# Twelve merged tiles turned by VectorE blocks and a DRAM round trip, and SyncE's queue written out by the planner

## The chip, the cores and the metric

The kernel runs on one core of a Trainium2 chip, in one launch. The metric is the device time of that core in microseconds (us). It was 1301.48 us before, the median of 3 runs from 1300.34 to 1301.94 us.

## The reference

One layer of a hybrid encoder on `x` of 512 tokens by 2048 features, in float32:

```python
hn = rmsnorm(x, norm_g)
proj = hn @ w_in                      # 12 q,k,v,gate groups of 4x128 columns, 4 forget logits, 3x2048 gate logits
gates = sigmoid(proj[gate columns] + b_gate)          # 3 branches x 2048
ya = forgetting_attention(...)        # 4 heads of 128: causal softmax with cumulative log forget bias
yb = chunked_relpos_attention(...)    # 4 heads: band of chunks with a learned relative bias
yc = stick_breaking_attention(...)    # 4 heads: causal, in log space
ys = stack(ya, yb, yc) * silu(gate)
up = einsum('bsnw,nwd->bsnd', ys, w_up)               # each branch 512 -> 2048
merged = sum(gates * up, over the 3 branches)
return x + merged @ w_out
```

`merged` is made with tokens on the partitions and columns on the free axis. The output projection contracts over the columns, so it needs them on the partitions: `merged` has to be turned.

## The kernel before

**Tiles and stages.** Every float32 product on PE is made of three products of split operands: a high part times the whole (high and low) of the other, and a low part times the high one. A weight block `raw` (128 partitions x 1024) is loaded by SyncE, its high part `wh` is made by ACT (L376), its low part `wl` by DVE (L386), and PE multiplies (L266). One such block is a *unit*: 12 matmuls of 512 columns in the Strassen-like projections, 24 in the others. `prep` readies units two ahead (`LA = 2`). There are 405 units in a row: the first head's group and gate group, then 11 heads of 28 units (attention of one head runs beside the projection of the next), then the up projections of 24 units, then the output projection of 2 x 28 units.

**The up stage.** `merged` has 4 column groups `g` of 512 columns and 4 token blocks `tb` of 128. The groups run in the order 0, 2, 1, 3. For each, three branches of two units are multiplied; `gates_of` loads the spilled gate logits (`sg<-gl`) and applies a sigmoid, `taken` multiplies and adds on DVE (L1323, L1330), and after the third branch `merged[g, tb]` is complete. `turned_m(g, i)` then makes the four tiles `m` of the group, each with 128 columns on the partitions and 512 tokens free: four PE transposes into one PSUM bank (L1357) and one copy on ACT (L1364). `merged_a` and `merged_b` make the operands of the output projection out of `m`: groups 0 and 1 give the `m1` operands, which the first units of the output projection read (group 0 first, group 1 from the fifth unit on); groups 2 and 3 are combined with them into `m2`, `m23` and `m4`.

**The heads' gate path.** `Head.gate` turns the gate columns of all heads but the last without PE: DVE transposes 32x32 blocks (L920), SyncE stores the tile to a DRAM scratch `gd` (L923), and ACT's queue issues four reads that put the blocks in place (L930). `silu` uses the result about ten units later.

**What sets the order.** A planner (`Flow`) simulates the work as generators: each yields an engine with a cost, an event to wait for, or slots of a buffer pool (`t2s`: 20 SBUF tiles, `raws`: 8 weight blocks, `atts` and `accs`: 4 PSUM banks each). The task that can start first, then the one due first, is taken and its instructions are emitted; that order is final on PE, ACT and DVE (`manual_schedule`). DMAs cost the planner nothing on an engine: `fetch` issues on SyncE and estimates the landing, `stored` estimates when a stored tile is free again. The order on SyncE's queue is not the planner's: the framework sets it. A queue issues in order, and an instruction that waits holds up what is behind it.

Of the kernel before, what the change touches and what calls it, by code (L numbers as in the profile page):

```python
# [15 lines left out]
P = 128  # L16
# [20 lines left out]
Q, K, V, G = 0, 1, 2, 3  # L37
PE, ACT, DVE = 0, 1, 2

# [25 lines left out]
class Flow:  # L65
# [4 lines left out]

    LATE = (0.3, 0.12, 0.12)

    def __init__(self):
        self.clock = [0.0] * 3
        self.idle = [0.0] * 3
        self.now = self.fin = 0.0
        self.tasks = []
# [86 lines left out]
def hybrid_kernel(  # L164
# [103 lines left out]

    line = [0.0, 0.0]

    def landing(ready, kb):

        line[0] = max(line[0], ready) + 0.5
        line[1] = max(line[1], line[0] + 1.0) + kb / 370.0
        return line[1] + 1.5

    def fetch(to, src, ready, kb):
        nc.sync.dma_start(to, src)
        return Event(landing(ready, kb))

    def add_up(to, src, ready, kb):
        nc.gpsimd.dma_start(to, src, accum_op=ALU.add)  # L282
        line[1] += kb / 250.0
        return Event(max(line[1], ready) + 6.5)

# [42 lines left out]
    for c in (0, 2):  # L328
# [18 lines left out]
    class Unit:  # L347
# [7 lines left out]
        def load(self):  # L355
            for s in self.srcs:
                yield raws, 1
                self.raw = raw_tile(self.shape)
                self.there.t = fetch(self.raw, s, flow.ready, 256 * self.shape[0]).t

# [192 lines left out]
    class Product(Unit):  # L553
# [6 lines left out]
        def load(self):  # L560
            task, p, c = self.task, self.p, self.c
            if p in (3, 6):
                return
            yield raws, 1
            self.raw = raw_tile()
            first, more = {1: ((0, 0), None), 2: ((0, 1), None), 4: ((1, 1), None),
                           5: ((1, 1), (1, 0)), 7: ((0, 0), (1, 0))}[p]
            ev = fetch(self.raw, task.src(*first, c), flow.ready, 512)
# [25 lines left out]
    class Strassen:  # L594
# [36 lines left out]
        def left(self, name, tb, op):  # L631

            if self.rest is None:
                set_(self.event(name, tb))
                return
            yield t2s, 1
            r = t2("xr")
            yield fetch(r, self.rest(name, tb), flow.now, 256)
# [76 lines left out]
    def forget_weights():  # L715

        yield t2s, 1
        t = t2("fw")
        yield fetch(t[:NH * KT, :2 * P], wfg, flow.now, 64)
        yield DVE, 0.25  # L720
        nc.vector.tensor_mul(t[:NH * KT, :P], t[:NH * KT, :P], t[:NH * KT, P:2 * P])
        nc.sync.dma_start(fwd.rearrange("h (k p) -> (h k) p", p=P), t[:NH * KT, :P])
        stored(t2s, 1, 32)
        fw_ev.t = flow.fin + 4.0

    def forget_sums(c, pair):

        yield f_sums[2 * c + pair - 1] if c + pair else fw_ev
        yield t2s, 2
        hs = range(2 * pair, 2 * pair + 2)  # L730
        ws = [t2("fb") for _ in hs]
        ev = [fetch(w, fwd[h:h + 1, c * S:(c + 1) * S].to_broadcast([P, S]), flow.now, 256) for w, h in zip(ws, hs)]
        yield t2s, 2
        xs_ = []

        def ahead(tb):
            x = t2("xf")
            t = fetch(x, xn[tb, c], flow.now, 256).t
            xs_.append((x, Event(max(ev[1].t, t) + FLATE)))

        ahead(0)
        ahead(1)
        for tb in range(QB):
            x, there = xs_[tb]
            yield there
            yield atts, 1
            for w, h, to in zip(ws, hs, (att(), x)):
                yield DVE, dve_us(S) + 0.12
                nc.vector.tensor_tensor_reduce(out=to, in0=x, in1=w, scale=1.0, scalar=0.0, op0=ALU.mult, op1=ALU.add,
                                               accum_out=fl[:, tb, h, c:c + 1])  # L750
                if to is not x:
                    give(atts)
            if tb + 2 < QB:
                ahead(tb + 2)
            else:
                give(t2s)
        give(t2s, 2)
        set_(f_sums[2 * c + pair])

    def forget_bias():  # L760
# [19 lines left out]
        give(atts)  # L780
        nc.sync.dma_start(fd.rearrange("b h p -> (b h) p"), t[:T, :P])
        stored(t2s, 1, 16)
        for h in range(NH):
            nc.sync.dma_start(v[32 * h:32 * (h + 1), :], fd[:, h, :].rearrange("b (c t) -> b c t", t=T))
        yield Event(flow.fin + 8.0)
        q = 0.15
# [19 lines left out]
        nc.vector.tensor_add(v, v, p)  # L806
        nc.sync.dma_start(fd2.rearrange("h (c t) -> (h c) t", t=T), v)
        f2_ev.t = flow.fin + 3.0

# [7 lines left out]
    class Head:  # L817
# [95 lines left out]
        def gate(self):  # L913
            yield from self.all_there()
            yield t2s, 1
            if not self.last:
                t = t2("gt")
                for tb in range(QB):
                    yield DVE, 0.3
                    nc.vector.transpose(t[:, blk(tb)], self.c[tb][:, blk(G)])  # L920
                self.taken()
                gd = dp.tile([4 * QB, 32, P], F32, name=nm("gd"))
                nc.sync.dma_start(gd.rearrange("(t a) r c -> (a r) t c", a=4), t.rearrange("p (t c) -> p t c", t=QB))  # L923
                stored(t2s, 1, 256)
                yield Event(flow.fin + 12.0)
                yield t2s, 1
                yield ACT, 0.2
                t = self.t[G] = t2("g")
                for b in range(4):
                    nc.scalar.dma_start(t[32 * b:32 * (b + 1), :].rearrange("p (n c) -> p n c", c=32),  # L930
                                        gd.rearrange("n r (b c) -> b r n c", c=32)[b])
                self.event(G).t = flow.fin + 14.0
                return
# [20 lines left out]
        def soft_start(self):  # L954
# [3 lines left out]
            if n == A:  # L958
                yield f2_ev
                b = self.bias = t2("cr")  # L960
                ev = fetch(b, fd2[self.h:self.h + 1, :].to_broadcast([P, S]), flow.now, 256)
                yield ev
# [3 lines left out]
            else:  # L966
                self.bias = t2("tb")
                ev = fetch(self.bias, rel[self.h], flow.now, 256)
                yield ev
# [125 lines left out]
        def av(self, j):  # L1095
# [23 lines left out]
            if not self.last:  # L1119
                yd[self.n, self.h] = dp.tile([P, S], F32, name=nm("yd"))  # L1120
                nc.sync.dma_start(yd[self.n, self.h], self.y)
                stored(t2s, 1, 256)

# [25 lines left out]
    def brow(i):  # L1149
        yield t2s, 1  # L1150
        b = brows[i] = t2("bg")
        brow_ev[i].t = fetch(b, b_gate[i:i + 1, :].to_broadcast([P, S]), flow.now, 256).t

    brows, brow_ev, brow_used = {}, {i: Event() for i in range(NB * NQ)}, {}

    def spill(i, tb, c, src):
# [9 lines left out]
        gl[key] = dp.tile([P, S], F32, name=nm("gl"))  # L1166
        nc.sync.dma_start(gl[key], c)
        stored(t2s, 1, 256)

# [107 lines left out]
    def split_y(i):  # L1277
        def go():
# [6 lines left out]
            else:  # L1285
                yield heads[i].event("y")
                yield t2s, 1
                t = t2("yr")
                yield fetch(t, yd[n, h], flow.now, 256)
            yield from split(ys[i].hi, ys[i].lo, two(t), S, y_ev[i])  # L1290
# [9 lines left out]
    def gates_of(n, g, tb):  # L1300
        yield last_head.event("hl", 2)
        yield t2s, 1
        t = sig[n, g, tb] = t2("sg")
        yield fetch(t, gl[n, g, tb], flow.now, 256)
        yield last_head.event("g")
# [42 lines left out]
    kept_m, m1_ev, mus = {}, [Event() for _ in range(UK)], {}  # L1348

    def turned_m(g, i):  # L1350
        for tb in range(QB):
            yield merged_ev[NB - 1, g, tb]
# [12 lines left out]
        give(atts)  # L1365
        k = 4 * g + i
        if k < UK:
            kept_m[k] = m
            spawn(merged_a(k, m), 4.0, flow.fin)
        else:  # L1370
            spawn(merged_b(k - UK, m), 3.0, flow.fin)

# [47 lines left out]
    for g in (0, 2, 1, 3):  # L1420
# [40 lines left out]
    def loads():  # L1461
        def x(kt):
# [4 lines left out]
            xraw[kt] = t2("x")  # L1467
            x_in[kt].t = fetch(xraw[kt], xT[kt], 0.0, 256).t

        def n(i):  # L1470
            n_in[i].t = fetch(xnat[i // 2][:, i % 2, :], xn[i // NQ, i % NQ], 0.0, 256).t

# [6 lines left out]
        for kind, i in order:  # L1479
            if kind == "x":  # L1480
                yield from x(i)
            elif kind == "n":
                n(i)
            else:
                yield from units[i].load()
# [18 lines left out]

    line[0] = 0.8
    flow.fin = 4.0
# [14 lines left out]
NR = 8  # L1521

OFF = dict(cs=4, ct=12, co=14, s=8, t=14, o=16, s1=3, t1=4, o1=5)
FAT, FGAP, FLATE = 44, 15, 3.5
# [49 lines left out]
```

## Time and profile before

| What | us |
|---|---|
| median of 3 runs | 1301.48 |
| the runs | 1301.48, 1300.34, 1301.94 |
| span of the profiled execution | 1300.1 |
| PE busy in it | 1294.1 |
| DVE busy | 1069.5 |
| ACT busy | 748.2 |
| POOL busy | 92.0 |

The page gives the profiled execution's time as its span, from first to last instruction; what lies around it is not listed, and the runs lie 0.2 to 1.8 us above it. Matmuls are pipelined and overlap, so a row's mean duration (about 390 ns for one of 512 columns) is longer than the distance from one to the next. "PEld" is PE's weight load, "SPq" SyncE's queue, "ACTq" the queue of ACT. In a row of waits stand the waiter, the releaser, then us in total, times and the longest. In a row of DMA issues stand the transfer, its queue, the count, the KB of each and the median us from issue to landing. The granted clock was 1.000 throughout.

### The profile page before, as it was taken

To read this page: it belongs to the slowest core of one execution; us is meant where nothing else is said; L and a number is where in the kernel's file an instruction comes from. 1 tells how busy PE (TensorE), PEld (TensorE's weight loads), DVE (VectorE), ACT (ScalarE), POOL (GpSimd) and SP (SyncE) were. 2 spreads that over 40 slices of the span, in tenths; PEclk is the share of its full clock that TensorE was granted. 3 is DMA by queue.
4 is the path that set the end of the run, shared out by engine and by line. 5 is a ranking of instruction groups with operands and counts; after the bars stand their busy time and mean duration, and the time that the engine had idled before them with its cause. 6 is when DMAs were issued, how large, how long until landed. Compare 5 with 4: busy or idle time off the path is not lost.

```text
span 1300.1 us, 17368 instructions
## 1 busy us (share of the span) xinstructions
PE 1294.1 (100%) x5941; PEld 1075.1 (83%) x5941; DVE 1069.5 (82%) x1607; ACT 748.2 (58%) x1259; POOL 92.0 (7%) x116
## 2 busy tenths in 40 slices
PE   9999999999999999999999999999999999999998
PEld 8888888888888888888888888888888888888887
DVE  7966797898989888898886886978879668698767
ACT  7745465565557646576466664666658546463442
POOL 0001000110011001110011000110000000000110
PEclk9999999999999999999999999999999999999999
DMA  9855687896788989888787777877796756738983
GB/s 358 256 147 145 185 230 194 230 239 215 218 238 237 250 236 272 236 240 240 205 249 175 222 213 191 252 162 208 224 282 194 264 194 196 177 93 258 250 245 126
DMA packets 124072, 284.39 MB, mean 219 GB/s; under 512 B 34368, under 2 KB 40144, under 8 KB 123984
## 3 DMA queue, kind: packets, MB, share of 16 engines
q1 hardware_dynamic: 83328, 221.42, 50.7%
q0 software_dynamic: 14976, 54.53, 23.1%
q10 hardware_dynamic: 25680, 7.34, 2.3%
q8 instruction: 46, 0.75, 0.2%
q14 instruction: 42, 0.34, 0.1%
HBM read 260.66 MB, written 22.59 MB: 218 GB/s over the span
## 4 chain that ended last, share of the span: by engine, by line
PE 99%; DMA 1%; DVE 0%; issue 0%; ACT 0%; ACTq 0%
PE acc L266 93%; PE att L1019 1%; PE att L873 1%; DMA gl<-u 1%; PE att L1109 1%; PE att L1108 1%; PE att L261 1%; PE att L262 1%; PE att L263 1%; PE att L1357 1%; PE att L1107 1%; PE att L430 0%; DVE s L702 0%; DVE u L1161 0%; DVE gt L920 0%
## 5 line engine op out<-in xcount | busy, mean ns | idle before, releaser
L376 ACT ACTIVATE wh<-raw 128x1024 fp32r<-128x1024 f32 (+1 forms) x404 | 426.9, 1057 | 412.6 <-PE acc L266 317.6
L386 DVE TENSOR_TENSOR wl<-raw,wh 128x1024 fp32r<-128x1024 f32 (+1 forms) x405 | 492.6, 1218 | 159.1 <-PE acc L266 110.6
L266 PE MATMUL acc<-wh,x 128*128 128x512 f32 x1664 | 428.7, 392 | 0.1
L266 PEld LDWEIGHTS acc<-wh,x 128*128 128x128 f32 x1664 | 310.2, 188 | 62.8 <-issue 0.3
L266 PE MATMUL acc<-wh,t 128*128 128x512 f32 x1056 | 272.4, 391 | 0.0
L266 PE MATMUL acc<-wl,x 128*128 128x512 f32 x832 | 230.7, 391 | 0.0
L266 PEld LDWEIGHTS acc<-wh,t 128*128 128x128 f32 x1056 | 197.1, 188 | 40.3
L266 PEld LDWEIGHTS acc<-wl,x 128*128 128x128 f32 x832 | 155.4, 188 | 32.3 <-DVE wl L386 0.2
L266 PE MATMUL acc<-wl,t 128*128 128x512 f32 x528 | 148.0, 392 | 0.0
L282 POOL DMA_DIRECT2D raw<-in_w_col x88 | 76.1, 865 | 867.6 <-ACT wh L376 209.0
L588 DVE TENSOR_TENSOR raw<-raw,raw 128x1024 f32<-128x1024 f32 x104 | 126.4, 1218 | 0.1
L266 PEld LDWEIGHTS acc<-wl,t 128*128 128x128 f32 x528 | 98.3, 188 | 19.7
L266 PE MATMUL acc<-wh,m 128*128 128x512 f32 x448 | 112.9, 389 | 0.0
L266 PE MATMUL acc<-wh,y 128*128 128x512 f32 x384 | 103.1, 390 | 0.0
L266 PEld LDWEIGHTS acc<-wh,m 128*128 128x128 f32 x448 | 84.1, 188 | 17.4
L266 PEld LDWEIGHTS acc<-wh,y 128*128 128x128 f32 x384 | 72.0, 188 | 15.0
L266 PE MATMUL acc<-wl,m 128*128 128x512 f32 x224 | 62.5, 390 | 0.0
L266 PE MATMUL acc<-wl,y 128*128 128x512 f32 x192 | 59.5, 391 | 0.0
L266 PEld LDWEIGHTS acc<-wl,m 128*128 128x128 f32 x224 | 41.9, 188 | 8.8 <-DVE wl L386 0.2
L266 PEld LDWEIGHTS acc<-wl,y 128*128 128x128 f32 x192 | 35.8, 188 | 7.1
L247 ACT ACTIVATE ah<-att 128x512 fp32r<-128x512 f32 (+3 forms) x48 | 20.9, 436 | 31.7 <-PE att L1019 31.6
L1323 DVE TENSOR_TENSOR sg<-acc,sg 128x512 f32<-128x512 f32 x48 | 32.9, 690 | 5.0 <-PE acc L266 2.6
(182 smaller groups left out, 1119.9 us busy)
## 6 DMA issues: line engine op xcount, KB each, us to landing
raw<-in_w_col SPq DMA_DIRECT2D x235, 512.0 KB, 5.0
raw<-in_w_col POOLq DMA_DIRECT2D x88, 512.0 KB, 8.2
raw<-in_w_out SPq DMA_DIRECT2D x40, 512.0 KB, 4.1
raw<-in_w_up SPq DMA_DIRECT2D x24, 512.0 KB, 3.8
sg<-gl SPq DMA_DIRECT2D x48, 256.0 KB, 4.8
xf<-in_xn SPq DMA_DIRECT2D x32, 256.0 KB, 6.7
raw<-in_w_out POOLq DMA_DIRECT2D x16, 512.0 KB, 6.5
gl<-u SPq DMA_DIRECT2D x22, 256.0 KB, 9.9
```

Of the source, the lines that this page charges most:

```text
L247: nc.scalar.activation(hi, src, AF.Copy)
L261: nc.tensor.matmul(ps, lh, rh, start=start, stop=False, skip_group_check=more)
L262: nc.tensor.matmul(ps, lh, rl, start=False, stop=False, skip_group_check=more)
L263: nc.tensor.matmul(ps, ll, rh, start=False, stop=stop, skip_group_check=more)
L266: nc.tensor.matmul(ps, w, x, start=start, stop=stop, skip_group_check=more)
L282: nc.gpsimd.dma_start(to, src, accum_op=ALU.add)
L376: nc.scalar.activation(u.hi, u.raw, AF.Copy)
L386: nc.vector.tensor_sub(u.lo, u.raw, f(u.hi))
L588: nc.vector.tensor_add(to.raw, to.raw, self.raw)
L873: nc.tensor.transpose(ps[:, blk(tb)], self.c[tb][:, blk(r)], identf)
L1019: nc.tensor.transpose(ps[:, blk(i)], self.p[i][:, blk(j)], identf)
L1323: nc.vector.tensor_mul(t, ps[tb], t)
```

## The change

Two things are changed. First, the merged tiles of groups 0, 2 and 1 (`DRAMS`) go the way of the heads' gates: DVE transposes the 32x32 blocks in place (`folded`), SyncE stores the tile to a DRAM scratch `md`, and when all four token blocks are there, `turned_m` reads each of the four tiles `m` back with four DMAs. Group 3 keeps the transposes on PE, now in `spun_m`. Second, SyncE becomes a fourth engine of the planner: every load and store on it is yielded with a cost of 0.37 us (0.54 for a read of `back`), emitted in the planner's order, and that order is final. The heads' four gate reads move from ACT's queue to SyncE's, and the landing estimates are new.

```diff
-PE, ACT, DVE = 0, 1, 2
+PE, ACT, DVE, SP = 0, 1, 2, 3
...
-    def landing(ready, kb):
-        line[0] = max(line[0], ready) + 0.5
-        line[1] = max(line[1], line[0] + 1.0) + kb / 370.0
-        return line[1] + 1.5
-    def fetch(to, src, ready, kb):
+    def landing(ready, kb):
+        line[0] = max(line[0], ready + 1.0) + kb / 370.0
+        return line[0] + (LAND if ready > 20.0 else 1.6)
+    def fetch(to, src, kb):
+        yield SP, 0.37
         nc.sync.dma_start(to, src)
-        return Event(landing(ready, kb))
+        return Event(landing(flow.fin, kb))
+    def store(to, t, kb, slots=None, n=1):
+        yield SP, 0.37
+        nc.sync.dma_start(to, t)
+        ev = Event(landing(flow.fin, kb))
+        if slots is not None:
+            slots.free += [ev.t] * n
+        return ev
+    def back(to, src):
+        n = src.shape[0] * 4
+        for b in range(4):
+            yield SP, 0.54
+            nc.sync.dma_start(to[32 * b:32 * (b + 1), :].rearrange("p (n c) -> p n c", c=32),
+                              src.rearrange("t (a r) c -> (t a) r c", r=32)[:, :, 32 * b:32 * (b + 1)]
+                              .rearrange("n r c -> r n c"))
+        return Event(landing(flow.fin, n * 32) + PIECES)
...
     ctx.enter_context(tc.manual_schedule(engines={mybir.EngineType.PE, mybir.EngineType.Activation,
-                                                  mybir.EngineType.DVE}))
+                                                  mybir.EngineType.DVE, mybir.EngineType.SP}))
...
-                nc.sync.dma_start(gd.rearrange("(t a) r c -> (a r) t c", a=4), t.rearrange("p (t c) -> p t c", t=QB))
-                stored(t2s, 1, 256)
-                yield Event(flow.fin + 12.0)
+                ev = yield from store(gd.rearrange("(t a) r c -> (a r) t c", a=4), t.rearrange("p (t c) -> p t c", t=QB), 256, t2s)
+                yield Event(ev.t + LATER)
                 yield t2s, 1
-                yield ACT, 0.2
                 t = self.t[G] = t2("g")
-                for b in range(4):
-                    nc.scalar.dma_start(t[32 * b:32 * (b + 1), :].rearrange("p (n c) -> p n c", c=32),
-                                        gd.rearrange("n r (b c) -> b r n c", c=32)[b])
-                self.event(G).t = flow.fin + 14.0
+                self.event(G).t = (yield from back(t, gd.rearrange("(t a) r c -> t (a r) c", a=4))).t
...
+    def folded(g, tb):
+        yield merged_ev[NB - 1, g, tb]
+        m = merged[g, tb]
+        yield DVE, dve_us(S) + 0.07
+        nc.vector.transpose(m, m)
+        if g not in md:
+            md[g] = dp.tile([QB, P, S], F32, name=nm("md"))
+        md_ev[g, tb].t = (yield from store(md[g][tb], m, 256, t2s)).t + LATER
     def turned_m(g, i):
+        for tb in range(QB):
+            yield md_ev[g, tb]
+        yield t2s, 1
+        m = t2("m")
+        yield (yield from back(m, md[g][:, :, blk(i)]))
+        arrived(g, i, m)
+    def spun_m(g, i):
         for tb in range(QB):
             yield merged_ev[NB - 1, g, tb]
...
         for i in range(QB):
-            at(len(units) - 1, lambda g=g, i=i: turned_m(g, i))
+            if g in DRAMS:
+                at(len(units) - 1, lambda g=g, i=i: folded(g, i))
+                at(len(units) - 1 + MSKIP, lambda g=g, i=i: turned_m(g, i))
+            else:
+                at(len(units) - 1, lambda g=g, i=i: spun_m(g, i))
...
+DRAMS = (0, 2, 1)
+MLATE, MSKIP = 2.5, 1
+LATER = 2.5
+LAND, PIECES = 2.5, 1.5
```

The remaining lines of the diff turn every other `fetch` and store (`x`, weights, gate biases, forget weights, `yd`, `yr`, `gl`, `sg`, `xr`) into the yielded form; `arrived` holds the lines that stood at the end of the old `turned_m`.

More of the change, by code (lines that the diff above doesn't have):

```diff
@@ L65 @@
 class Flow:
-    LATE = (0.3, 0.12, 0.12)
+    LATE = (0.3, 0.12, 0.12, 0.0)
     def __init__(self):
-        self.clock = [0.0] * 3
-        self.idle = [0.0] * 3
+        self.clock = [0.0] * 4
+        self.idle = [0.0] * 4
         self.now = self.fin = 0.0
@@ L358, in load @@
                 self.raw = raw_tile(self.shape)
-                self.there.t = fetch(self.raw, s, flow.ready, 256 * self.shape[0]).t
+                self.there.t = (yield from fetch(self.raw, s, 256 * self.shape[0])).t
         def split_done(self):
@@ L567, in load @@
                            5: ((1, 1), (1, 0)), 7: ((0, 0), (1, 0))}[p]
-            ev = fetch(self.raw, task.src(*first, c), flow.ready, 512)
+            ev = yield from fetch(self.raw, task.src(*first, c), 512)
             if more is not None:
@@ L637, in left @@
             r = t2("xr")
-            yield fetch(r, self.rest(name, tb), flow.now, 256)
+            yield (yield from fetch(r, self.rest(name, tb), 256))
             yield DVE, dve_us(S)
@@ L731, in forget_sums @@
         ws = [t2("fb") for _ in hs]
-        ev = [fetch(w, fwd[h:h + 1, c * S:(c + 1) * S].to_broadcast([P, S]), flow.now, 256) for w, h in zip(ws, hs)]
+        ev = []
+        for w, h in zip(ws, hs):
+            ev.append((yield from fetch(w, fwd[h:h + 1, c * S:(c + 1) * S].to_broadcast([P, S]), 256)))
         yield t2s, 2
@@ L737, in ahead @@
             x = t2("xf")
-            t = fetch(x, xn[tb, c], flow.now, 256).t
+            t = (yield from fetch(x, xn[tb, c], 256)).t
             xs_.append((x, Event(max(ev[1].t, t) + FLATE)))
-        ahead(0)
-        ahead(1)
+        yield from ahead(0)
+        yield from ahead(1)
         for tb in range(QB):
@@ L753, in forget_sums @@
             if tb + 2 < QB:
-                ahead(tb + 2)
+                yield from ahead(tb + 2)
             else:
@@ L806, in forget_bias @@
         nc.vector.tensor_add(v, v, p)
-        nc.sync.dma_start(fd2.rearrange("h (c t) -> (h c) t", t=T), v)
-        f2_ev.t = flow.fin + 3.0
+        f2_ev.t = (yield from store(fd2.rearrange("h (c t) -> (h c) t", t=T), v, 8)).t
     def tri(name, dt=F32):
@@ L960, in soft_start @@
                 b = self.bias = t2("cr")
-                ev = fetch(b, fd2[self.h:self.h + 1, :].to_broadcast([P, S]), flow.now, 256)
+                ev = yield from fetch(b, fd2[self.h:self.h + 1, :].to_broadcast([P, S]), 256)
                 yield ev
@@ L967, in soft_start @@
                 self.bias = t2("tb")
-                ev = fetch(self.bias, rel[self.h], flow.now, 256)
+                ev = yield from fetch(self.bias, rel[self.h], 256)
                 yield ev
@@ L1120, in av @@
                 yd[self.n, self.h] = dp.tile([P, S], F32, name=nm("yd"))
[L1121 to L1122 removed]
+                yield from store(yd[self.n, self.h], self.y, 256, t2s)
         def stages(self):
@@ L1166, in spill @@
         gl[key] = dp.tile([P, S], F32, name=nm("gl"))
-        nc.sync.dma_start(gl[key], c)
-        stored(t2s, 1, 256)
+        yield from store(gl[key], c, 256, t2s)
     def quad(parts, g, done, early=False):
@@ L1288, in go @@
                 t = t2("yr")
-                yield fetch(t, yd[n, h], flow.now, 256)
+                yield (yield from fetch(t, yd[n, h], 256))
             yield from split(ys[i].hi, ys[i].lo, two(t), S, y_ev[i])
@@ L1303, in gates_of @@
         t = sig[n, g, tb] = t2("sg")
-        yield fetch(t, gl[n, g, tb], flow.now, 256)
+        yield (yield from fetch(t, gl[n, g, tb], 256))
         yield last_head.event("g")
@@ L1482, in loads @@
             elif kind == "n":
-                n(i)
+                yield from n(i)
             else:
@@ L1503, in stream @@
                 spawn(u.after(), 0.0, flow.fin)
-    line[0] = 0.8
+    flow.clock[SP] = 0.8
     flow.fin = 4.0
```

43 lines of the change are left out of this document (23 added, 20 removed).

## The prediction

> **What bounds the kernel now.** I read the page's busy times first, then the chain that ended last in order of time, then who waited for whom on PE, then the DMA issues and SyncE's order around one head.
>
> ```profile
> span 1300.1 us, 17368 instructions
> PE 1294.1 (100%) x5941; PEld 1075.1 (83%) x5941; DVE 1069.5 (82%) x1607; ACT 748.2 (58%) x1259; POOL 92.0 (7%) x116
> ...
> PE 99%; DMA 1%; DVE 0%; issue 0%; ACT 0%; ACTq 0%
> ```
>
> PE is busy all but 6.0 us of the span. A busy PE could still hide small gaps, because matmuls overlap, so the chain and the waits must say whether it is fed:
>
> ```profile
> 1.13 4.02 PE att L430 x36
> ...
> 1011.70 1.39 PE acc L266 x6
> ...
> 1042.87 32.69 PE acc L266 x144
> ...
> 1296.33 0.02 issue
> 1296.35 0.69 DVE s L702
> ```
> ```profile
> PE att L430 <- DVE mskf L302: 1.1, 1, 1.1
> PE att L261 <- ACT p L1049: 0.9, 1, 0.9
> ```
>
> 32.69 us for 144 projection matmuls is 227 ns for one; 6 in 1.39 us, between attention pieces, are 232 ns. So the matmuls follow each other at one rate from 5.25 us on, and PE waits by name only 0.9 us after its start. The span is warm-up (5.2), PE's own list of work, and a tail of 3.8 us (1300.1 less 1296.33). Only work taken from PE's list, or a new wait of PE, can move the end. The other engines matter when they become late for PE.
>
> **The change part by part.** (1) For column groups 0, 2 and 1 the four calls of `turned_m` no longer transpose on PE: 16 transposes a group, 48 in all.
>
> ```profile
> 1041.13 1.75 PE att L1357 x16
> ...
> 1075.56 1.75 PE att L1357 x16
> ...
> 1109.97 1.75 PE att L1357 x16
> ...
> 1144.18 1.75 PE att L1357 x16
> ```
>
> Each piece of the chain is 16 transposes in 1.75 us (109 ns each), with matmuls directly before and after. Three of four go: 3 x 1.75 = 5.25 us off PE's list. The fourth, group 3 at 1144.18, stays on PE.
>
> (2) With them go 12 copies out of PSUM on ACT:
>
> ```profile
> L1364 ACT ACTIVATE m<-att x16: 592/597/621, 1041.6 to 1146.1; 128x512 f32<-128x512 f32 x16
> L251 DVE TENSOR_TENSOR m<-m,m x16: 679/682/694, 1043.8 to 1165.7; 128x512 fp32r<-128x512 f32 x16
> L1378 DVE TENSOR_TENSOR m<-m x8: 418/422/426, 1042.2 to 1116.1; 128x256 f32<-128x256 f32 x8
> L247 ACT ACTIVATE m<-m x16: 613/616/632, 1043.1 to 1161.8; 128x512 fp32r<-128x512 f32 x16
> L920 DVE STREAM_TRANSPOSE gt<-w x20: 303/304/307, 162.7 to 905.3; 128x128 f32<-128x128 f32 x20
> ```
>
> 12 x 0.60 = 7.2 us less on ACT, worth nothing to the end, since ACT is idle 42%. (3) VectorE gets 12 block transposes of 128x512. No row has that size. Between one 512-column operation (0.68) and four of 128 columns (4 x 0.304 = 1.22) I take 0.70, since fixed cost is paid once: 8.4 us in all (8.2 to 14.6), 2.8 us per group. What covers it:
>
> ```profile
> 1041.13:1075.56 34.43, 34.43 (x162) 28.73 (x161) 24.44 (x35) 16.80 (x26) 0.00 (x0) 1.00 0.56 184
> 1075.56:1109.97 34.41, 34.41 (x163) 28.74 (x161) 30.40 (x51) 20.03 (x34) 1.73 (x2) 1.00 0.74 210
> 1109.97:1145.93 35.96, 35.96 (x177) 30.31 (x175) 25.43 (x37) 14.78 (x23) 1.73 (x2) 1.00 0.52 136
> 1145.93:1170.00 24.07, 24.07 (x107) 19.77 (x107) 24.07 (x36) 17.66 (x27) 2.34 (x3) 1.00 0.50 124
> ```
>
> (Length, then PE, PEld, DVE, ACT, POOL busy, clock, DMA share, GB/s.) Over the first three stretches DVE is busy 80.3 of 104.8 us; 8.4 more makes 88.7, or 85%. That fits, so I cost it at nothing. The cover is gone in the fourth stretch, where DVE is full: work that slides past 1146 would hold up PE by its own length.
>
> (4) Does it slide? Group 1, the last one through DRAM, has its merged tiles at about 1110. Then come four transposes (2.8 to 4.9), the store, sixteen reads issued on SyncE, the last landing, a subtraction and a split (0.42 + 0.62 + 0.68 = 1.7). The nearest rows for the DMAs are the heads' gate path, which makes the same trip already, and the `yd` store:
>
> ```profile
> raw<-in_w_col SPq DMA_DIRECT2D x235, 512.0 KB, 5.0
> ...
> gd<-gt SPq DMA_DIRECT2D x11, 256.0 KB, 11.6
> g<-gd ACTq DMA_DIRECT2D x44, 64.0 KB, 2.9
> yd<-y SPq DMA_DIRECT2D x11, 256.0 KB, 4.4
> ```
> ```profile
> 180.74 2.06 ACTq L930 DMA_DIRECT2D g<-gd  x4
> 183.02 1.06 ACT L376 ACTIVATE wh<-raw 128x1024 fp32r<-128x1024 f32 x1 [1.66 <-DMA g<-gd]
> ```
>
> Four reads take 2.06 us to issue, so sixteen take 8.2. At best 1110 + 2.8 + 4.4 + 8.2 + 2.9 + 1.7 = 1130; with the slow store 1110 + 4.9 + 11.6 + 8.2 + 2.9 + 1.7 = 1139. The output projection reads this group from its fifth unit on: 1145.9 + 4 units x 12 x 0.227 = 1156.8. That leaves 18 to 27 us, and 7 to 16 us to the full DVE stretch. Cost: nothing.
>
> (5) The heads' gate reads move from ACT's queue to SyncE's: 44 issues, 22.7 us less of ACT's queue (it held up `wh` above by 1.66), 22.7 more of SyncE's, with the 48 new reads (24.7) and 12 stores (about 0.4 each, 4.8). SyncE issues in order and now has its whole order written by the planner, so a read that waits for its store holds the weight loads behind it. The planner lets the read start 1.0 + 256/370 + 2.5 + 2.5 = 6.7 us after the store's issue if the line is free; the row says 11.6. Around one head SyncE does this:
>
> ```profile
> 149.73 14.83 SPq L278 DMA_DIRECT2D raw<-in_w_col  x6
> ...
> 170.46 0.45 SPq L923 DMA_DIRECT2D gd<-gt  x1
> 173.10 0.33 SPq L278 DMA_DIRECT2D raw<-in_w_col  x1
> 178.98 2.72 SPq L1167 DMA_DIRECT2D gl<-s  x2
> ```
> ```profile
> 189.22 23.14 SPq L278 DMA_DIRECT2D raw<-in_w_col  x5
> ```
>
> A read planned at 177.2 would wait to 182.1 (170.46 + 11.6) and be issued by 184.2. Behind it stand two stores, which only free tiles, and at 189.22 the next weight load, which waits for its buffer anyway. Five us of room: cost nothing.
>
> (6) The order of every engine's list is written anew, since four clocks now shape it. No row can show this. PE's list cannot gain more than the 0.9 us wait above, which may go. For the loss the nearest rows are weight loads that already wait for the low part:
>
> ```profile
> L266 PEld LDWEIGHTS acc<-wl,m 128*128 128x128 f32 x224 | 41.9, 188 | 8.8 <-DVE wl L386 0.2
> ...
> SPq L278 <- DVE wl L386: 468.9, 166, 13.0
> SPq L278 <- DVE raw L588: 335.6, 99, 15.9
> ```
>
> A named idle of 0.2 us says that margins are thin in places, but not crossed; SyncE itself waits 804 us for buffers, mostly with weights already ahead. I take 0 between a gain of 0.9 and a loss of one such crossing of 0.2 in each of 11 heads and the tail stages (about 3 us).
>
> **The sum.** 1300.1 less 5.25 is 1294.85. The three runs lie 0.2 to 1.8 us over the profiled span, the median 1.4 over it: 1296.2, or 0.40% less than 1301.48.
>
> **The rivals.** (a) Small new PE waits eat half or more of the gain. For it: DVE is full after 1146, and an operation of 1.2 us put before a `wl` there reaches PE. Against: every path above has microseconds of room. Three to six waits of about 1 us give 1296.2 + 4.5 = 1300.7; from 2.7 us on it is no change, by the bound of 0.2% (2.6 us) that a measurement of this kernel can tell.
>
> (b) Slower: SyncE's reads wait for their stores and starve the weights in every head. It decides from the point where the store lands after 170.46 + 16.7 = 187.2, since 2.06 us of issue then reach 189.2. Each us beyond, over 11 heads, costs up to 11 us; 2 us late gives 1296.2 + 22 = 1318. The longest landing known for this store is 12.8 us:
>
> ```profile
> DMA to landing us min/median/max: 10.3/11.6/12.8
> ```
>
> Against it stand those 4 us; for it, the gate reads and the loads now share one queue.
>
> (c) The reads with 128-byte runs are far slower than I take. One after the other at 2.9 us, group 1's sixteen end at 1110 + 4.9 + 11.6 + 46.4 = 1173; with 1.7 us that is 18 us after they are needed, so 1314. Against: the four reads at 180.74 are gone from the DMA engines by 185:
>
> ```profile
> 183.00:184.00 1.00, 1.00 (x6) 0.81 (x6) 0.88 (x2) 0.98 (x1) 0.00 (x0) 1.00 0.94 213
> 184.00:185.00 1.00, 1.00 (x6) 0.84 (x5) 1.00 (x1) 0.09 (x1) 0.00 (x0) 1.00 0.50 79
> ```
>
> They overlap, about 1 us each, so sixteen take about 17 us rather than 46. The Trainium skill speaks against the change here (VectorE: DVE Perf Modes, The three transpose paths): it sends a full 128x128 transpose to TensorE, and warns that a plain DMA that transposes by access-pattern strides is 19 times slower than the crossbar path. As an estimate by that factor alone, a tile that moves 256 KB in 0.7 us would take 13 us, twelve 160 us, and the end would come some 50 us later, near 1346; the head's four reads, over in about 4 us, disagree, since VectorE has turned the 32x32 blocks and whole 128-byte runs are moved.
>
> **How the numbers follow.** Forecast 70%, its own range 1295.0 to 1298.8. Rival (a) 14%, 1298.9 to 1304. Rival (b) 13%, rival (c) 3%, both slower. So faster 0.70, same 0.14, slower 0.16. The range runs from 1294.9 (5.25 and the 0.9, with a little for the runs' spread) up into (a), to 1303: 70 and about 11 in 100.
>
> **What the changed profile would show.** If right: L1357's successor has 16 transposes instead of 64, PE is busy about 1289 us, the projection matmuls still 227 ns apart, and at the three places of 1.75 us the chain runs on. Twelve DVE transposes near 0.70; twelve `m` tiles from `md` before 1146; weight loads after a gate read at most where they stood. If (a): pieces with named waits of PE or PEld for DVE `wl` or ACT `wh`. If (b): SyncE waits of over 5 us for `gd` or `md`, then `wh` waiting for `raw`, then PE for `wh`. If (c): landings of the reads of `md` far over 10 us and a gap of PE near the fifth unit of the output projection. The prediction is wrong if the new order of any list opens waits of PE that sum to over 2.7 us, wherever they stand.

## The result and the profile after

The changed kernel takes 1317.59 us (median; 1316.19 to 1318.57) against 1301.03 us for the kernel before on the same chip: a ratio of 1.0128, 95% interval 1.0113 to 1.0142. It is 16.6 us slower; the prediction was 1296.2, faster, with 1303.0 as its upper end. The profiled execution took 1318.57 us, with a span of 1316.9.

The page of the changed kernel: span, busy times, clock by slices, the chain by engine, and the two groups of PE with idle time before them (behind the last bar).

```profile
span 1316.9 us, 17329 instructions
...
PE 1296.1 (98%) x5893; PEld 1071.4 (81%) x5893; DVE 1072.9 (81%) x1619; ACT 743.5 (56%) x1247; POOL 91.7 (7%) x116
...
PEclk9999999999999999999999999999999899989999
...
PE 93%; DMA 3%; DVE 2%; SPq 1%; ACT 1%; issue 1%; DVEq 0%; ACTq 0%
...
L266 PE MATMUL acc<-wh,m 128*128 128x512 f32 x448 | 114.8, 394 | 7.3 <-DVE sg L1335 7.3
...
L266 PE MATMUL acc<-wh,y 128*128 128x512 f32 x384 | 105.6, 397 | 4.3 <-DVE sg L1335 4.2
```

PE has 48 instructions fewer (5941 to 5893), and yet its busy time rises by 2.0 us, while the span grows by 16.8. The chain is no longer PE at 99%: DMAs, DVE and SyncE's queue now carry 6% of it. Two slices of the clock line show an 8; the matmuls there take longer, by about 5 us in all, as the stretches below show. The waits of the changed kernel name the rest (waiter, releaser; us in total, times, longest), first PE's, then some of DVE's, then one of SyncE's queue:

```profile
PE acc L266 <- DVE sg L1335: 11.5, 3, 7.3
PE acc L266 <- DVE wl L407: 3.4, 4, 1.6
PE att L451 <- DVE mskf L323: 1.1, 1, 1.1
```
```profile
DVE m L1414 <- DMA m<-md: 14.0, 2, 9.7
...
DVE tb L985 <- DMA tb<-in_rel: 10.3, 4, 3.2
...
DVE cr L978 <- DMA cr<-fd: 6.0, 3, 2.4
```
```profile
SPq L297 <- DMA gd<-gt: 23.5, 11, 4.5
```

PE waits for `sg` of L1335 because that multiplication empties a PSUM bank: until DVE has done it, PE has nowhere to write. And DVE waits 14.0 us, in two places, for the tiles read back through DRAM. The timeline of DVE, then that of PE, at the larger of the two:

```profile
1141.57 0.69 DVE L1342 TENSOR_TENSOR sg<-sg,sg 128x512 f32<-128x512 f32 x1
1151.95 0.42 DVE L1414 TENSOR_TENSOR m<-m 128x256 f32<-128x256 f32 x1 [9.70 <-DMA m<-md]
...
1153.64 1.22 DVE L407 TENSOR_TENSOR wl<-raw,wh 128x1024 fp32r<-128x1024 f32 x1
1154.78 0.68 DVE L1335 TENSOR_TENSOR sg<-acc,sg 128x512 f32<-128x512 f32 x1
```
```profile
1147.63 0.61 PE L266 MATMUL acc<-wl,y 128*128 128x512 f32 x2
1155.51 3.78 PE L266 MATMUL acc<-wh,m 128*128 128x512 f32 x8 [7.26 <-DVE sg L1335]
```

DVE's order is fixed. A subtraction of the two halves of a read-back tile of group 1 (L1414) stands in it ahead of a `wl` and the `sg` multiplications of group 3, and the last read of that tile lands 9.70 us later than DVE gets there. PE fills its banks and stands still for 7.26 us. The eight matmuls that follow take 3.78 us, more than twice the 227 ns each.

Stretches of the changed kernel (length, then PE, PEld, DVE, ACT, POOL busy, clock, DMA share, GB/s). The first two lie around a wait of PE at the start of the up stage, the last after the wait just shown:

```profile
1020.30:1023.10 2.80, 0.04 (x1) 0.00 (x0) 2.25 (x4) 2.77 (x5) 0.00 (x0) 0.90 1.05 399
1023.20:1029.00 5.80, 5.78 (x14) 4.53 (x15) 2.36 (x4) 4.96 (x10) 0.00 (x0) 0.50 0.70 264
...
1155.00:1160.00 5.00, 4.49 (x12) 3.39 (x13) 5.00 (x10) 1.79 (x3) 0.00 (x0) 0.59 0.00 0
```

**The account.** To find are 16.8 us of span and the 5.25 that the transposes gave: about 22. PE's named waits grow by 14.7 (11.5 + 3.4 + 1.1, and 0.7 in two smaller rows, against 2.0 before). The two stretches at a clock of 0.50 and 0.59 lose 5.8 x 0.50 + 5.0 x 0.41 = 5.0. That is 19.7; no named wait accounts for the rest. Counted another way, by the distance from one matmul's start to the next beyond its own rate (227 ns, 109 for a transposition), where that is over 0.1 us too long, PE loses 2.3 us from 5 us on in the kernel before and 23.5 in the changed one. By place: 2.6 at 351 to 366, 6.0 at 1020 to 1029, 1.6 at 1074, 10.8 at 1141 to 1163, the rest in small pieces. This count is used below as "PE loses".

### The profile page after: what moved, and what is told of

Same layout as the page of the kernel before. It is cut to its first block, busy times and chain, and to the rows that moved or that the text cites. A ratio compares the mean times of both kernels' runs of the same rounds, so it can differ in the third digit from the quotient of the medians.

```text
span 1316.9 us, 17329 instructions
## 1 busy us (share of the span) xinstructions
PE 1296.1 (98%) x5893; PEld 1071.4 (81%) x5893; DVE 1072.9 (81%) x1619; ACT 743.5 (56%) x1247; POOL 91.7 (7%) x116
## 4 chain that ended last, share of the span: by engine, by line
PE 93%; DMA 3%; DVE 2%; SPq 1%; ACT 1%; issue 1%; DVEq 0%; ACTq 0%
PE acc L266 88%; DMA gd<-gt 1%; PE att L1033 1%; PE att L892 1%; DMA m<-md 1%; DMA sg<-gl 1%; DVE wl L407 1%; PE att L1123 1%; PE att L1122 1%; PE att L263 1%; PE att L262 1%; PE att L261 1%; PE att L1121 1%; SPq L297 1%; DVE sg L1335 0%
## 5 line engine op out<-in xcount | busy, mean ns | idle before, releaser
L1319 ACT ACTIVATE sg<-sg 128x512 f32<-128x512 f32 x48 | 28.4, 622 | 24.4 <-DMA sg<-gl 24.3
```

Source lines behind the costliest of these rows:

```text
L1319: nc.scalar.activation(t, t, AF.Sigmoid)
```

## The experiments

Two theories run through them. O: the trips themselves are sound, and the loss is a sum of faults in the planner's times and orders. D: the stretch from 1110 to 1150 has too little room on the DMA engines and SyncE's queue for the third trip. Later P (the rewritten lists of all engines cost) stands against Q (the order written for SyncE's queue costs).

**No trip at all.** Everything else of the change stays, and all four groups are turned on PE.

```diff
-DRAMS = (0, 2, 1)
+DRAMS = ()
```

> The changed kernel with SyncE's written order, but no group through DRAM (all four on PE). Theory O (the DVE's fixed order puts the work on a read-back tile before its reads have landed): the PE losses of 1.6 us near 1074 and 10.8 us near 1140 to 1163 vanish, 5.25 us of transposes come back, and the 6.0 us near 1020 and the 4 us in the heads stay, since they come from the order written anew: 1317.6 - 12.4 + 5.25 = about 1310. Rival D (the round trip is to blame for all): 1301. Rival S (SyncE's written order is to blame for all, the round trip for nothing): 1317.6 + 5.25 = 1323.

1310.75 us, ratio 1.0074 (1.0059 to 1.0089). So 9.9 us of the loss have nothing to do with the trips, and the trips add 6.8, although they take 5.25 off PE. PE loses 10.3 here, 3.2 of it at the same place as in the changed kernel, the start of the up stage.

**The trips alone.** The kernel before, with its planner, its landing estimates and the framework's order on SyncE's queue; the three groups go through DRAM, the reads stand on SyncE's queue, and the merged work is planned 14 us after the issue of the last read.

```diff
+        nc.vector.transpose(m, m)
+        nc.sync.dma_start(md[g][tb], m)
...
+        for b in range(4):
+            nc.sync.dma_start(m[32 * b:32 * (b + 1), :]..., src[:, :, 32 * b:32 * (b + 1)]...)
+        arrived(g, i, m, flow.fin + 14.0)
...
+DRAMS = (0, 2, 1)
```

> The kernel before, its SyncE queue left to the framework, with groups 0, 2 and 1 through DRAM, and the planner told that a tile's reads land 14 us after their issue. Theory O: the round trip does no harm when its landing is charged; the 5.25 us of PE are gained, less up to 2 us of new waits: 1296 to 1298. Rival D (128-byte reads fill the DMA engines, so the tiles are late whatever the planner is told): PE waits of 5 us or more between 1110 and 1160, 1301 or more.

1301.99 us, ratio 1.0008 (0.9998 to 1.0018): not the 1296 to 1298 of O, but no disaster either. PE loses 5.0, of it 2.1 at 1139. SyncE's queue and DVE there, and PE's largest wait, in this run:

```profile
1129.04 0.46 SPq L278 DMA_DIRECT2D sg<-gl  x1
1129.54 6.87 SPq L1372 DMA_DIRECT2D m<-md  x5
1136.51 0.50 SPq L278 DMA_DIRECT2D sg<-gl  x1
```
```profile
1138.09 0.69 DVE L1323 TENSOR_TENSOR sg<-acc,sg 128x512 f32<-128x512 f32 x1 [2.46 <-ACT sg L1307]
```
```profile
PE att L1392 <- DVE sg L1330: 1.7, 1, 1.7
```

Five reads keep the queue for 6.87 us, and group 3's last gate load, which is wanted first, stands behind them. That is not all: the gate for which DVE waits 2.46 us came by the load of 1129.04, ahead of the five, which landed only 8.3 us later, so a load is late beside the reads too. And the ten executions spread from 1299.21 to 1304.64, with the profiled one at 1299.80: those with a mean granted clock of 0.997 or 0.998 took 1301.66 or more, so part of what the median loses goes with the clock and isn't in this profile.

**Two trips, kernel before.** As the last, with `DRAMS = (0, 2)`: group 1 goes back to PE.

> The kernel before, with only groups 0 and 2 through DRAM (landing of the reads charged 14 us), group 1 and 3 on PE, SyncE's queue left to the framework. Theory O and D together: no urgent read is left, so the waits of 2.1 and 0.9 us between 1127 and 1142 of the run with three groups go, and 3.5 us of transposes are gained: 1297.5, faster than before. Rival: two groups still crowd SyncE's queue and sg loads come late: 1300 to 1302.

1299.06 us, ratio 0.998 (0.997 to 0.9989): faster than both kernels. The page and PE's waits of this run:

```profile
span 1296.5 us, 17374 instructions
...
PE 1291.1 (100%) x5909; PEld 1071.2 (83%) x5909; DVE 1072.7 (83%) x1615; ACT 744.9 (57%) x1251; POOL 91.7 (7%) x116
```
```profile
PE att L430 <- DVE mskf L302: 1.1, 1, 1.1
PE acc L266 <- DVE wl L386: 0.4, 2, 0.2
```

32 transposes are worth 3.5 us by the sum of the prediction; the span falls by 3.6 (1300.1 to 1296.5) and PE loses 2.3 as before. Between medians the gain is only 2.2.

**The third trip with the loads ahead.** As the three trips alone, and group 3's last gate loads are asked for two units earlier.

```diff
-at(len(units) - (3 - tb // 2 if g or b else 2), ...gates_of(n, g, tb))
+at(len(units) - (3 + (g == 3 and b == 2) * 2 - tb // 2 if g or b else 2), ...gates_of(n, g, tb))
```

> The kernel before with all three groups through DRAM, as in the run that took 1301.99, with one edit: the sigmoid loads of group 3's last branch are wanted two units (about 11 us) earlier, so that its last load stands ahead of the last five reads of group 1 on SyncE's queue, where it stood behind them. Theory O (in that kernel the third trip fails only because those loads stand behind the reads): the 2.1 us that PE lost at 1139 go, 1302.0 - 2.1 = 1299.9, and if the smaller losses near 1127 and 1155 go with them, 1298.4. Theory D (in that stretch the DMA engines are full, so whatever is put first, something else comes late): PE still loses 2 us or more between 1120 and 1160, at weights or at the reads instead, 1301 to 1303.

1299.22 us, ratio 0.9987 (0.9977 to 0.9996). O gave 1299.9 for this. SyncE's queue in that stretch, the same wait of PE, and the page's busy times:

```profile
1130.10 2.61 SPq L278 DMA_DIRECT2D sg<-gl  x1
1132.81 6.07 SPq L1372 DMA_DIRECT2D m<-md  x6
```
```profile
PE att L1392 <- DVE sg L1330: 1.0, 1, 1.0
```
```profile
PE 1288.9 (99%) x5893; PEld 1068.0 (82%) x5893; DVE 1073.8 (83%) x1619; ACT 742.7 (57%) x1247; POOL 91.9 (7%) x116
```

The last load now goes out at 1130.10, ahead of six reads, and the 1.7 that PE waited at L1392 becomes 1.0. Between the medians of the two runs lie 2.8 us, of which the two profiles show this 0.7. So the third trip fits too when those loads are asked for earlier, though D keeps a part: the load of 1130.10 still takes 2.61 us to issue, PE still waits 1.0, and the third trip gains nothing that can be measured over two.

**Two trips, changed kernel.** `DRAMS = (0, 2)`, all else as changed.

> The changed kernel with groups 0 and 2 through DRAM and group 1 back on PE. Theory O: only the last group's tiles are urgent, so the 10.8 us between 1140 and 1163 vanish and 1.75 us come back: 1317.6 - 10.8 + 1.75 = about 1308.5; the 1.6 us near 1074 may stay. Rival S: the losses are in the heads and at the start of the up stage and around SyncE's order there: 1317 or more.

1307.17 us, ratio 1.0058 (1.0041 to 1.0075), within 1.4 of what was expected. The third trip costs the changed kernel 10.4 us. The first two, beside the run without any, give 3.6. That 32 transposes should give 3.5 is no more than agreement: both runs have four executions that spread over some 4 us, and in this one DVE still waits 4.3 us for a read-back tile.

**The landing charged.** In the changed kernel the merged work is planned from the end of the read's issue; here from the estimated landing plus 5 us.

```diff
-        yield (yield from back(m, md[g][:, :, blk(i)]))
-        arrived(g, i, m)
+        ev = yield from back(m, md[g][:, :, blk(i)])
+        arrived(g, i, m, ev.t + 5.0)
```

> The changed kernel, with one edit: the work on a read-back tile is ready in the planner at the landing estimate of its four reads plus 5 us, and no more at the end of their issue. Theory O: DVE has other work ahead of the late tiles, the waits of DVE for the reads (4.3 and 9.7 us) shrink to under 3 us together, the PE losses of 1.6 and 10.8 us to under 4: 1317.6 - 9 = about 1308. Rival D: the reads land as late as before and PE waits for the operands instead, near the fifth unit of the output projection: 1314 or more.

1311.48 us, ratio 1.0084 (1.0063 to 1.0104): 6.1 less than the changed kernel, short of the 1308 of O. DVE's wait for `m<-md` is gone from the waits, but the time comes back in part another way, as the chain, then DVE's timeline and PE's waits of this run show:

```profile
1132.09 8.86 DMA m<-md
1141.01 7.38 DMA sg<-gl
```
```profile
1141.00 0.69 DVE L1335 TENSOR_TENSOR sg<-acc,sg 128x512 f32<-128x512 f32 x1 [4.64 <-ACT sg L1319]
```
```profile
PE acc L266 <- DVE sg L1335: 7.5, 2, 4.6
```

A read's DMA, and after it a load of `sg`, now end last. PE waits up to 4.6 us for a multiplication that itself stood 4.64 us for its gate: a gate load comes late among the reads.

**SyncE's order left to the framework.** The run without trips, and SyncE is taken out of `manual_schedule`; the planner still plans its loads.

> No group through DRAM, and the planner as in the changed kernel (SyncE as a fourth engine, new landing estimates), but SyncE's queue itself is ordered by the framework again; PE, ACT and DVE keep the planned lists. Theory P (the loss of 10 us without any round trip comes from the new lists of DVE and ACT, which the new estimates make): the time stays at 1308 to 1312. Rival Q (it comes from the order on SyncE's queue): 1301 to 1304.

1307.59 us, ratio 1.0048 (1.0033 to 1.0063), mostly as P said: the fixed order on SyncE's queue costs about 3.2 of the 9.9 (the two intervals just overlap). The rest lies in the lists of the other engines and in the heads' gate reads, which stay on SyncE's queue here too; no run parts these two. One row of SyncE's waits in this run speaks to rival (b):

```profile
SPq L297 <- DMA gd<-gt: 69.6, 11, 10.8
```

SyncE stands three times as long for the heads' stores as in the changed kernel (23.5), and still this run is the faster one.

**The landing estimate.** The run without trips, with the 1.5 us that the kernel before assumes from a transfer's end to its use.

```diff
-LAND, PIECES = 2.5, 1.5
+LAND, PIECES = 1.5, 1.5
```

> No group through DRAM, SyncE's order written, and one number changed: the planner's landing estimate LAND is 1.5 us and no more 2.5. Theory P: tiles come free 1 us earlier in the planner, the last head's second transposition gets its two tiles earlier, and the loss at the start of the up stage (3.15 us near 1022 in the run without round trips) goes: 1307 to 1308; the losses in the heads stay. Rival: an earlier estimate makes the waits for stores that have not landed longer, and the time rises to 1312 or more.

1304.39 us, ratio 1.0029 (1.0019 to 1.0039): 6.4 less, twice what was expected. The wait at the start of the up stage is gone, and so are several small losses of PE in the heads. That 1 us of caution for each transfer makes tiles free later in the plan and so pushes the attention work back is argued from the code, not shown; that the estimate sets these waits is shown.

**The start of the up stage filled.** The changed kernel with 27 matmuls of no use put before the second unit of the up stage, so that PE is idle for less time there; they are not part of the computation.

> The changed kernel, with 27 matmuls of 128x128 whose result nobody reads (27 x 107 ns = 2.9 us) put on PE where it waits 2.9 us at the start of the up stage. Theory G (the granted clock falls to 0.5 because PE stood idle there, and the 14 matmuls at 427 ns cost another 3 us): with PE busy in the wait the clock stays at 1.0, the loss of 6.0 us falls to about 3, 1317.6 - 3 = 1314.5. Rival: the clock falls for another reason, the time stays at 1317.6 or rises by up to 2.9.

1316.01 us, ratio 1.0109 (1.0094 to 1.0124). The same two stretches, in this run:

```profile
1020.30:1023.10 2.80, 1.42 (x11) 1.14 (x8) 2.25 (x4) 2.79 (x6) 0.00 (x0) 1.00 1.06 391
1023.20:1029.00 5.80, 5.80 (x27) 4.78 (x26) 2.36 (x4) 5.33 (x10) 0.00 (x0) 1.00 0.53 202
```

27 matmuls start in the second stretch instead of 14, at a clock of 1.00. So half of the 6.0 us lost there was the clock and not the wait. The filling is only a partial one: the 27 matmuls take 1.7 us rather than the 2.9 expected, and PE still waits 1.4 there. Of the 3 us expected only 1.6 reach the end, within what the two intervals leave open; PE's later waits for L1335 are longer (12.1 - 1.4 = 10.7 here, 11.5 - 2.9 = 8.6 without).

**Both mendings.** The changed kernel with the landing charged and `LAND` at 1.5, first with all three groups, then with two.

> All three groups still go through DRAM; the merged work is planned at the estimated landing of its read plus 5 us, and the planner's landing estimate for every other transfer is 1.5 us as in the kernel before. Theory O (the slowdown is a sum of planning faults: the start of the up stage, the early subtraction, and the reads' own load on SyncE's queue and the DMA engines): the 4.7 us lost near 1020 in the charged kernel vanish, 1311.5 - 4.7 = 1306.8, and PE still loses about 7 us between 1130 and 1150 because group 3's sigmoid loads stand behind the reads. Theory D (the third trip itself cannot be covered whatever the planning): the same number, and the loss after 1130 is what is left. If the landing estimate has nothing to do with the up stage's start: 1311.

> As the three-group kernel with both mendings, but only groups 0 and 2 go through DRAM, so group 1's sixteen reads do not stand ahead of group 3's loads. Without the trip of any group, and with the same landing estimate, the time was 1304.4; two groups take 32 transposes or 3.5 us off PE. Theory O: 1304.4 - 3.5 = 1300.9, no named wait of PE above 2 us after 1070. Theory D: 1300.9 as well, since the third trip is gone. If the first two trips also cost SyncE's queue something here: 1303 to 1305.

With three groups 1305.82 us, ratio 1.0043 (1.0026 to 1.006), where 1306.8 was expected: the 4.7 us at 1020 are gone, and PE still loses 5.5 between 1134 and 1145. With two groups 1302.26, ratio 1.0005 (0.9996 to 1.0015), where 1300.9 was expected; no wait of PE is over 1.6.

**And the heads' tables.** The last, and the loads of the heads' bias tables (`tb`, `cr`), for which DVE stood 10.3 and 6.0 us in the changed kernel, are planned 5 us later.

```diff
                 ev = yield from fetch(self.bias, rel[self.h], 256)
-                yield ev
+                yield Event(ev.t + 5.0)
```

(The same for `cr`.)

> As the two-group kernel with both mendings, and the heads' bias loads (the tables of relative positions) are planned 5 us later than the landing estimate, since VectorE was seen to stand behind them in the heads. Theory: the 1.5 us lost near 600 and the smaller losses of the heads go, 1300.9 - 1.5 = 1299.4. If the heads' losses come from the gate reads in SyncE's queue and not from the tables: 1300.9 as without it. If every rewriting of the lists opens some new wait: 1302 or more.

1300.84 us, ratio 0.9996 (0.9986 to 1.0005): 1.4 less, the step that was expected, from a higher start; the intervals overlap, so that this step isn't certain. DVE's waits for `tb` and `cr` no longer stand among its ten largest. The ladder from the changed kernel is then 1317.6, 1311.5 (landing charged), 1305.8 (`LAND`), 1302.3 (no third trip), 1300.8 (tables). Three rungs are times in the plan; the third trip's is the room that its reads take on SyncE's queue and the DMA engines. The ladder ends level with the kernel before, and 1.8 above the same two trips planned by the old planner; what these last 2 us are, no run settled.

## Why the prediction was wrong

Two steps of the prediction failed, both put at nothing in its sum. Step 4 said that the trips' lateness costs nothing: the trips add 6.8 us where they should have taken 5.25 off, so it cost 12.1. Step 6 took 0 for the new order, 3 at most: it cost 9.9 together with the moved gate reads.

**Step 1 was right, as near as the runs tell.** PE loses 21.2 us more than before while the span grows by 16.8: the difference is 4.4 of the 5.25, and in the kernel before the two trips alone gave 3.6 of span, though 2.2 between medians, for a predicted 3.5. The PE busy time of about 1289 that the prediction named as the sign of a right forecast is not in the changed kernel (1296.1), but it is in the kernel before with all three trips and the loads ahead (1288.9), with the same 5893 instructions on PE.

**Step 3 was right in size and wrong in what it stands for.** The 128x512 transposition takes the 0.70 that I took between 0.68 and 1.22. The tile `sg` of the changed kernel (first the 16 transposes that stay on PE, then DVE's twelve):

```profile
L1398 PE MATMUL att<-identf,sg x16: 270/272/273, 1164.0 to 1165.7; 128*128 128x128 f32 x16
L1368 DVE STREAM_TRANSPOSE sg<-sg x12: 668/702/707, 1046.8 to 1120.7; 128x512 f32<-128x512 f32 x12
```

DVE's share of busy time was no bound. It was late because it stood, not because it was full: from 1142 on it did nothing for 9.7 us. The step's own condition, that nothing slides past the end of the up stage (1146 in the kernel before), is what broke.

**Step 4 failed first.** I asked when group 1's tiles are there, 1130 to 1139, and when the output projection reads them, 1156.8, and called the difference room. Three things were wrong with that. The trip was longer: the last transposition began at 1120.7, where I had it done by 1114.9 (PE's losses up to there had shifted the stage), and the sixteen reads, with 8.2 us of SyncE's queue in my sum, were spread over 24.7. Its timeline in the changed kernel, then the reads' line as a group:

```profile
1126.12 0.32 SPq L297 DMA_DIRECT2D m<-md  x1
...
1129.82 2.92 SPq L297 DMA_DIRECT2D m<-md  x4
1132.84 2.28 SPq L278 DMA_DIRECT2D sg<-gl  x1
...
1138.20 3.77 SPq L297 DMA_DIRECT2D m<-md  x3
1142.07 2.07 SPq L278 DMA_DIRECT2D sg<-gl  x1
...
1145.46 5.32 SPq L297 DMA_DIRECT2D m<-md  x5
```
```profile
L297 SPq DMA_DIRECT2D m<-md x48: 318/487/2353, 1061.3 to 1149.1; - x48
...
DMA to landing us min/median/max: 3.1/4.6/8.1
```

From the first at 1126.12 to the end of the last at 1145.46 + 5.32 = 1150.78 is 24.7, with six gate loads and two weight loads in between; the reads' own issues are some 14 of it. The prediction held a nearer figure, about 17 us for sixteen reads, under its rival (c), and did not use it in this step. Second, the time that counts was not when PE reads the tile but where DVE's list has the subtraction: with an order fixed by the plan, an operation that is planned too early blocks the urgent ones behind it, and its reader's due time says nothing. Third, the diff shows the cause, and I read past it: `turned_m` waits for the reads' landing, but `arrived` then gives `flow.fin`, the end of the issue, as the time from which the merged work may be planned. The old line was right for a copy on ACT and is wrong for a DMA. Charging the landing took DVE's wait away and 6.1 us with it.

**Step 5 held, for its own reason.** SyncE waits for the heads' stores at most 4.5 us in the changed kernel and 10.8 in a faster one, so weights were not starved there, and rival (b), though its 1318 is by chance within half a microsecond of the result, was not what happened. What the move of the heads' gate reads costs by itself, no run shows. The reads do hold up what stands behind them, but in the up stage, where the loads behind them are gate loads that DVE and PE wait for.

**Step 6 was under-sized more than threefold.** I bounded the new order of all lists at +3; without any trip it cost 9.9. My bound took one crossing of 0.2 in each head from the waits of the kernel before. But those waits are the outcome of one set of estimates, and `LAND` alone, 1 us for each transfer, moved the time by 6.4. And a wait of PE can cost more than its length.

**The rivals.** (a) had the right kind (new waits of PE for DVE) at a fifth of its size. (c) is not borne out as it stood: the reads land in 3.1 to 8.1 us, several under way at once, and in the kernel before with two trips neither PE nor DVE nor ACT waits for them. But in the changed kernel they are slower than the 2.9 us that I took, and group 1's sixteen needed 26 us from the first issue to the last landing, near 1152. The factor of 19 that the Trainium skill (VectorE: DVE Perf Modes, The three transpose paths) gives for a plain DMA that transposes by strides, where the innermost stride at the destination is large, is not seen in any run of this trip: by the prediction's estimate of 13 us a tile from that factor, group 1's four tiles alone would need 52.

## What to carry to other kernels

Where each engine's order is fixed by a plan, ask of every new operation not when its result is needed but whether its operands can be there at the place it gets in its engine's list, and what stands behind it; an operation that becomes ready by a DMA has to be charged with the landing, not the issue. A change of the planner's estimates is a change of the whole kernel: measure it alone before putting anything on top. Transfers that may be late go behind the ones that are wanted first on the same queue; here that order decided whether the kernel with the third trip lay level with two trips or, between medians, 3 us above.

## What the runs showed of the hardware

**The same wait costs 3 or 6 us, by the clock.** In the changed kernel PE waited 2.88 us at 1020, and the granted clock then stood at 0.50 until about 1029: 14 matmuls start in 5.8 us where 27 do at full clock:

```profile
1023.22 2.07 PE L266 MATMUL acc<-wh,y 128*128 128x512 f32 x4 [2.88 <-DVE sg L1335]
```

The run without trips has a wait of the same length there, and no drop (PE's timeline, then stretches, of that run):

```profile
1025.50 1.20 PE L266 MATMUL acc<-wh,y 128*128 128x512 f32 x4 [2.88 <-DVE sg L1335]
```
```profile
1022.00:1024.00 2.00, 0.63 (x5) 0.44 (x3) 1.78 (x3) 1.98 (x2) 0.00 (x0) 1.00 1.03 389
1024.00:1026.00 2.00, 0.50 (x2) 0.46 (x3) 1.45 (x4) 1.99 (x5) 0.00 (x0) 1.00 1.06 398
1026.00:1028.00 2.00, 2.00 (x10) 1.61 (x10) 1.84 (x4) 2.00 (x5) 0.00 (x0) 1.00 1.05 402
```

The profile shows one execution, with a mean clock of 1.000; the three others of the same kernel have 0.997 and 0.998. The mean doesn't tell where, but it fits a drop that comes in some executions and not in others. The Trainium skill (TensorE: Matmul & The Clock Gate, Part 1: The HAM clock gate) says that the clock is halved after an idle window of about 3.4 us, and that the windows run free of the kernel. That the same gap is sometimes caught and sometimes not agrees with free windows; that 2.88 us were enough does not agree with the length.

**Issuing on SyncE is not a fixed price.** A read of 64 KB in 128-byte runs takes 0.49 us to issue in the median and up to 2.35; the long ones stand where the DMA engines are full. The changed kernel in two such stretches (the next to last number is the DMA share):

```profile
1132.00:1138.00 6.00, 6.00 (x29) 4.95 (x28) 5.87 (x11) 4.03 (x8) 0.86 (x1) 1.00 1.20 227
...
1142.00:1146.00 4.00, 4.00 (x19) 3.30 (x18) 0.26 (x1) 0.46 (x1) 0.00 (x0) 1.00 1.20 221
```

They move fewer bytes (221 to 227 GB/s) than the stretch at 1020 (399), at a fuller share. From 1132 to 1138, 2606 of 2922 packets are under 512 bytes, at 1020 68 of 610. That points to short runs costing the engines time rather than bytes, though other transfers run beside the reads. The planner's 0.54 us for such a read fits the median and is up to more than four times too low here.
